# A hybrid decoder block: a third output tile in attention, another order of PSUM banks, two copies' engine, and a Newton step in two operations

## The chip, the cores and the metric
The kernel runs on one core of a Trainium2 chip. The metric is the device time of one execution in microseconds (us). Three executions of the kernel before took 2113.8, 2116.68 and 2114.82 us: a median of 2114.82.

The core's engines run side by side, each through its own list of instructions in order: TensorE (PE, matmuls; its weight loads are shown apart as PEld), VectorE (DVE), ScalarE (ACT), GpSimd (POOL) and SyncE (SP), which here only issues DMAs. ACT and POOL issue DMAs as well.

## The reference
One layer of a decoder block over 2048 positions of width 1024, in float32:

```python
proj = x @ w_in + b_in                      # q, k, v, g_attn, u_lru, g_lru, gate_logits
q, k = rope(q), rope(k)                     # 3 head groups of 8 heads, 64 wide
for g, (window, dilation) in enumerate(((128, 1), (512, 4), (2048, 16))):
    o_g, lse_g = dilated_band_attention(q[:, :, g], k[:, :, g], v[:, :, g], window, dilation)
attn = sum(softmax(lse over g) * o_g) * silu(g_attn)
y_a = attn @ w_attn_proj
u = causal_depthwise_conv(u_lru, conv_w, conv_b)
h = rg_lru(u, ...)                          # block-diagonal gates, a scan over the positions
y_b = (h * silu(g_lru)) @ w_lru_proj
merged = sigmoid(gates[0]) * y_a + sigmoid(gates[1]) * y_b
out = merged @ w_out + b_out
x = layer_norm(alpha * x + out, ln_gain, ln_bias)
```

In each group the positions are regrouped by their residue modulo the dilation, and each block of 128 queries sees its own block of keys and the one before it, cut to a band. For group 2 (dilation 16) there is only one block in each residue, so no block before.

## The kernel before, in words
All five engines' lists are written in program order: the schedule is by hand, and an instruction that waits holds up everything behind it on its engine. Products that need float32 accuracy are done as three matmuls of a high and a low part. `later(n, fn)` puts a step off by `n` rounds; `run(late)` runs what has come due.

**In-projection (to about 1444 us).** Blocks of `x` and of the weights are combined into seven products for eight; one product after the other runs in a ring of `q` tiles (L622) in the first four PSUM banks, those of the pool `ps` that come first; behind them lie the tags `t` and `g`, two banks each. After each product `evacuate` sums it into `y` tiles (DVE, L227), and chains of further steps go on with them: `qk_chain` with the rotation, others with `v`, and `mg_chain` with the merge gates, a `tanh` and a store to `mg_scr`. The SBUF tiles of 2 KB a partition for all of these are 32 slots `s0` to `s31`, taken by `take` and returned by `give`. `take` picks the slot that has been vacant the longest, but for names with `y` in the last step of the plan it goes by the list `LATE` first, each of its slots once; these `y` tiles are the last merge gates', which ACT stores (L386).

**Attention (about 1444 to 1655 us).** The SBUF and the PSUM of the in-projection are released and taken anew by the pools `p_p`, `at_p`, `Y` and `aps`. There are 12 units, one for each head pair `hp` and group, in the order of groups 0, 2, 1; each has four rounds of four query blocks, 48 rounds (`NG`) in all. For round `i`:

- `scores(i)`: matmuls into four `s` tiles, a PSUM bank each (L1005), two at a time. In the first round of a unit it also takes the unit's statistics tile `sta` (three buffers in turn) and its output tile `ot` (8 KB a partition, two buffers in turn).
- `peak`: DVE adds the mask, writes `p` and keeps the row's largest value in `sta` (L1012, eight in a round). `expo`: ACT takes the exponential of `p` and its sum (L1020, eight).
- `turn`: PE transposes `p` into tiles `pt` with the PSUM tag `t`, a bank each (L1030). `bring`: copies of these from PSUM to `ptb` in SBUF, four in a round, by ACT (L1043) or by DVE (L1045). `light` says whether DVE does the one of them that is otherwise ACT's in the second half of the round.
- `values`: matmuls of `ptb` with the values into `o`, of the tag `t` too (L1058).
- `leave`: DVE copies `o` to the unit's `ot` (L1067 in group 0, L1071 in group 2, L1069 in group 1). A round later SP issues the stores: of groups 0 and 1 each quarter of `ot` to `o_scr` (L1073), of group 2 the whole tile once at the end of the unit (L1075); and at the end of each unit the statistics to `st_scr` (L1080, 1082, and for group 1 four at L1085).

The four `s` tiles take four banks and the tag `t` the other four; which of them come first follows from which tag is asked for first. Rounds overlap: the loop's turn `i` holds the scores of round `i`, the second half of the softmax of `i - 1`, `values(i - 2)` and `leave(i - 3)`, in an order that is written out. The loop has three turns without scores at the end (`i` from 48 to 50). Beside it the next units' queries, keys and values are loaded and split in two by POOL (L811), and the last rounds load `h` and the first weights of the next stage.

**Last stages (about 1655 to 2112 us).** The pool `fp` takes PSUM: `y` of four banks for the two projections (`yb`, L1310 to L1312, and `ya`, L1388 to L1390), `ct` of one and `z` of three for the combination of the groups and the out-projection. `out_job` runs 16 times: PE makes `z` from `merged` and `wo` (L1420 to L1422), DVE adds the residual, takes mean and variance; ACT takes a square root, DVE the reciprocal and one Newton step for 1/sqrt(variance + eps) on one column of `mv` (L1451 to L1453), scales and shifts `x` (L1457), and the row is stored. At the end of the last one only DVE, ACT and the stores are left.

Of the kernel before, what the change touches and what calls it, by code (L numbers as in the profile page):

```python
# [8 lines left out]
F32 = mybir.dt.float32  # L9
F32R = mybir.dt.float32r  # L10
AF = mybir.ActivationFunctionType
ALU = mybir.AluOpType
# [3 lines left out]
P = 128  # L16
S = 2048
# [3 lines left out]
CH = 512  # L21
# [10 lines left out]
def hybrid_block_kernel(ctx: ExitStack, tc: tile.TileContext, a: dict, out: bass.AP):  # L32
    nc = tc.nc
    sp, act, dve, pool, pe = nc.sync, nc.scalar, nc.vector, nc.gpsimd, nc.tensor
# [90 lines left out]
    sl_p = stA.enter_context(tc.tile_pool(name="sl_p", bufs=1))  # L125
    ps = stA.enter_context(tc.tile_pool(name="ps", bufs=2, space=PSUM))
    NS, NL = 32, 4
    LATE = [31, 7, 8, 9, 30]
    TRACE = False
    vacant = list(range(NS))  # L130
    home = {}
# [416 lines left out]
    light = [("v", FT_V + 2 * j, FT_V + 2 * j + 1) for j in range(6)]  # L548
# [157 lines left out]
    for s, pl in enumerate(plan):  # L706
        if pl[4] == "ug" and not (pl[0] and pl[1][1][0] - FT_U in put_off):
            at(base[s] + 1, lambda i=pl[1][1][0] - FT_U: fetch_gr(i))
        if pl[0] and pl[4] == "ug":
            i = pl[1][1][0] - FT_U  # L710
# [38 lines left out]
    def bring(t, b, c):  # L749

        at(t - 3, lambda: [keep_raw(b, c, kk) for kk in K4])
        at(t, lambda: [one_block(b, kk) for kk in K4])
# [36 lines left out]
    def unit(u):  # L789

        return (0, 2, 1)[u % 3], u // 3
# [170 lines left out]
    at_p = stB.enter_context(tc.tile_pool(name="at_p", bufs=2, reuse_waits="tile"))  # L962
    Y = stB.enter_context(tc.tile_pool(name="Y", bufs=1, reuse_waits="tile"))
    aps = stB.enter_context(tc.tile_pool(name="aps", bufs=2, space=PSUM, reuse_waits="tile"))
    def prev(g, n):
        if g == 0:
            return n - 1 if n >= 1 else None
        if g == 1:
            return n - 4 if n >= 4 else None
        return None  # L970
# [3 lines left out]
    sta, ot = {}, {}  # L974
# [6 lines left out]
    def scores(i):  # L981
        u, q = divmod(i, 4)
        g, _ = unit(u)
        A, B = units[u]
        if q == 0:
            sta[u] = p_p.tile([P, 16, 4], F32, tag="sta", name=f"sta{u}", bufs=3)
            ot[u] = at_p.tile([P, S], F32, tag="ot", name=f"ot{u}")
        for w in range(2):
            s = st["s", i, w] = [aps.tile([P, 2, 256], F32, tag="s", name=f"s{i}{w}{h}", bufs=4) for h in range(2)]
            for j in range(2):  # L990
                n = 4 * q + 2 * w + j
                lo = first(i, 2 * w + j)
                for x, y in ((0, 0), (1, 0), (0, 1)):
                    for h, hs in enumerate(HALF):
                        K = B[hs, y]
                        if g == 2:
                            k = K.rearrange("p (c r j) -> p r c j", c=4, r=16)[:, n]
                        elif lo:
                            k = K[:, n * P:(n + 1) * P]
                        elif g == 0:  # L1000
                            k = K[:, (n - 1) * P:(n + 1) * P]
                        else:
                            c, r = divmod(n, 4)
                            k = K[:, (c - 1) * CH:(c + 1) * CH].rearrange("p (c r j) -> p r c j", c=2, r=4)[:, r]
                        pe.matmul(s[h][:, j, lo:256], A[hs, x, n * P:(n + 1) * P], k, start=(x + y == 0), stop=(y == 1))  # L1005
# [109 lines left out]
    NG = 48  # L1115
# [4 lines left out]
    for i in range(NG + 3):  # L1120
        u = i // 4
        on, turns = i < NG, 0 < i <= NG
        run(late)
        if i in VORD:
            loads += v_parts(*VORD[i])
        if i % 4 == 0 and 1 <= u <= 9:
            loads += unit_parts(u + 2)
        for _ in range(2):
            if loads:
                loads.pop(0)()  # L1130
        copied = 1 < i <= NG + 1
        light = copied and (unit((i - 2) // 4)[0] == 2 or i % 3 == 1)
        if on:
            scores(i)
        if i > 2:
            leave(i - 3)
        if copied:
            bring(i - 2, 1, 1, dve)
            if light:
                bring(i - 2, 1, 0, dve)  # L1140
        if turns:
            expo(i - 1, 2, 1)
        if copied and not light:
            bring(i - 2, 1, 0, act)
        if turns:
            expo(i - 1, 3, 0)
            expo(i - 1, 3, 1)
        if on:
            peak(i, 0, 0)
            expo(i, 0, 0)  # L1150
            for j, h in ((0, 1), (1, 0), (1, 1)):
                peak(i, j, h)
        if turns:
            turn(i - 1, 0)
            bring(i - 1, 0, 0, act)
            bring(i - 1, 0, 1, dve)
        if on:
            for j, h in ((0, 1), (1, 0), (1, 1)):
                expo(i, j, h)
            peak(i, 2, 0)  # L1160
            peak(i, 2, 1)
        if i > 1 and i - 2 < NG:
            values(i - 2)
        if turns:
            turn(i - 1, 1)
        if on:
            peak(i, 3, 0)
            peak(i, 3, 1)
            expo(i, 2, 0)
        if i in (40, 41):  # L1170
            prep_wl(i - 40, 2)
        if 42 <= i < 46:
            load_h(0, 2 * (i - 42), 2)
            load_h(0, 2 * (i - 42) + 1, 2)
        if i in (46, 47):
            prep_wl(i - 44, 2)
        now["n"] += 1
# [7 lines left out]
    Z = ctx.enter_context(tc.tile_pool(name="Z", bufs=1, reuse_waits="tile"))  # L1185
    rc_p = ctx.enter_context(tc.tile_pool(name="rc_p", bufs=4, reuse_waits="tile"))
    fp = ctx.enter_context(tc.tile_pool(name="fp", bufs=2, space=PSUM, reuse_waits="tile"))
    stC = ctx.enter_context(ExitStack())
    cb_p = stC.enter_context(tc.tile_pool(name="cb_p", bufs=3, reuse_waits="tile"))
    wt_p = stC.enter_context(tc.tile_pool(name="wt_p", bufs=1, reuse_waits="tile"))  # L1190
# [218 lines left out]
    def out_job(tt):  # L1409
        rows = slice(tt * P, (tt + 1) * P)  # L1410
        x = XR.pop(tt)
        mh, ml = MS.pop(tt)
        last = tt == 15
        parts = [slice(0, CH), slice(CH, CH + 256), slice(CH + 256, D)] if last else [slice(0, CH), slice(CH, D)]
        zz = [fp.tile([P, CH], F32, tag="z", name=f"z{tt}{n}", bufs=3)[:, 0:hs.stop - hs.start] for n, hs in enumerate(parts)]
        for k0, k1 in ((0, 6), (6, 8)) if tt == 0 else ((0, 8),) if tt % 4 else ((0, 7), (7, 8)):
            for z, hs in zip(zz, parts):
                for k in range(k0, k1):
                    w = WO[k]
                    pe.matmul(z, mh[:, k], w[:, 0, hs], start=(k == 0), stop=False)  # L1420
                    pe.matmul(z, mh[:, k], w[:, 1, hs], start=False, stop=False)  # L1421
                    pe.matmul(z, ml[:, k], w[:, 0, hs], start=False, stop=(k == 7))  # L1422
        if tt + 1 < 16:
            load_xr(tt + 1)
            split_m(tt + 1, slice(0, 8 if (tt + 1) % 4 else 7))
        if tt == 1:
            for fn in at1:
                fn()
        dve.scalar_tensor_tensor(out=x, in0=x, scalar=ALPHA, in1=vec[0], op0=ALU.mult, op1=ALU.add)
        st_ = cst.tile([P, 4, 6], F32, tag="st", name=f"st{tt}", bufs=2)  # L1430
        n = 0
        for z, hs in zip(zz, parts):
            dve.tensor_tensor(out=x[:, hs], in0=x[:, hs], in1=z, op=ALU.add)
            step = 256 if last else CH
            for q in range(hs.start, hs.stop, step):
                dve.bn_stats(out=st_[:, n, :], in_=x[:, q:q + step])
                n += 1
        mv = cst.tile([P, 4], F32, tag="mv", name=f"mv{tt}", bufs=2)
        dve.bn_aggr(out=mv[:, 0:2], in_=st_[:, 0:n])
        act.activation(mv[:, 2:3], mv[:, 1:2], AF.Sqrt, bias=epst)  # L1440
        halves = (slice(0, CH), slice(CH, D))

        def centre(hs):
            dve.scalar_tensor_tensor(out=x[:, hs], in0=x[:, hs], scalar=mv[:, 0:1], in1=vec[1][:, hs],
                                     op0=ALU.subtract, op1=ALU.mult)

        centre(halves[0])
        dve.reciprocal(out=mv[:, 2:3], in_=mv[:, 2:3])

        dve.tensor_scalar(out=mv[:, 1:2], in0=mv[:, 1:2], scalar1=EPS, scalar2=-0.5, op0=ALU.add, op1=ALU.mult)  # L1450
        dve.tensor_tensor(out=mv[:, 3:4], in0=mv[:, 2:3], in1=mv[:, 2:3], op=ALU.mult)  # L1451
        dve.tensor_scalar(out=mv[:, 3:4], in0=mv[:, 3:4], scalar1=mv[:, 1:2], scalar2=1.5, op0=ALU.mult, op1=ALU.add)
        dve.tensor_tensor(out=mv[:, 2:3], in0=mv[:, 2:3], in1=mv[:, 3:4], op=ALU.mult)  # L1453
        for hs, eng in zip(halves, (sp, act) if last else (act, act)):
            if hs.start:
                centre(hs)
            dve.scalar_tensor_tensor(out=x[:, hs], in0=x[:, hs], scalar=mv[:, 2:3], in1=vec[2][:, hs],  # L1457
                                     op0=ALU.mult, op1=ALU.add)
            eng.dma_start(out[rows, hs], x[:, hs])
# [96 lines left out]
```

## Time and profile before
| | |
|---|---|
| median of the three executions | 2114.82 us (2113.8 to 2116.68) |
| the profiled execution | 2113.77 us |
| its span in the trace | 2112.0 us |
| granted TensorE clock, mean | 0.997 |
| busy PE | 2088.6 us (99%) |
| busy DVE | 1663.8 us (79%) |
| busy ACT | 1120.5 us (53%) |
| busy POOL | 491.9 us (23%) |
| moved by DMA | 524.69 MB, 248 GB/s on average |

The time of an execution is that of the whole program; the span runs from the first to the last record of the trace, and the difference, 1.8 us here, lies around it. An engine's busy time counts the instructions that compute; waiting and issuing are not in it. The table by windows gives for each stretch the same busy times, so that a stage can be read apart from the whole, with the clock that TensorE was granted (1.00 is full speed). A row of an instruction has its start in us from the beginning of the span, its length, its engine and line, what it writes and reads by the program's names, and in brackets how long the engine stood idle just before it and what ended that. "L1071" is line 1071 of the kernel before; in the changed kernel the lines behind the in-projection stand one to three further down.

### The profile page before, as it was taken

The page shows a single profiled execution, that of the slowest core. Times are in us where ns is not written, and L with a number is a line of the kernel's source. Part 1 is how long each engine was busy: PE and PEld are TensorE (multiplying, and loading weights), DVE is VectorE, ACT ScalarE, POOL GpSimd, SP SyncE. Part 2 cuts the span into 40 slices and gives each one's busy share as a digit, 9 for nine tenths or more (in the row PEclk, how much of TensorE's full clock was granted, in tenths as well). Part 3 has the DMA queues.
Part 4 walks back from the last instruction along what each step waited for, and adds up shares of the span by engine and source line. Part 5 has one row for each costly group of instructions (what it writes and reads, how often), then busy time and mean ns, then how long its engine had stood idle before and what let it go on. Part 6 is the DMA issues. An engine that isn't in the chain of part 4 may idle for free.

```text
span 2112.0 us, 35853 instructions
## 1 busy us (share of the span) xinstructions
PE 2088.6 (99%) x12016; PEld 1729.0 (82%) x12016; DVE 1663.8 (79%) x3193; ACT 1120.5 (53%) x2348; POOL 491.9 (23%) x465
## 2 busy tenths in 40 slices
PE   8999999999999999999999999999999999999998
PEld 7888888888888888887888888888989888888887
DVE  8987888888888867787787887877989645576667
ACT  6356456457356565656567666667999411221100
POOL 1111111111111002231232232222536444331120
PEclk9999999999999999999999999999999999999999
DMA  8987997997997976677788788879998788864432
GB/s 271 268 273 223 276 284 209 284 289 234 273 291 237 329 221 200 213 238 212 249 252 274 255 251 269 257 223 382 296 303 263 238 283 274 302 245 155 161 110 70
DMA packets 345832, 524.69 MB, mean 248 GB/s; under 512 B 124208, under 2 KB 153904, under 8 KB 341808
## 3 DMA queue, kind: packets, MB, share of 16 engines
q1 hardware_dynamic: 325760, 489.54, 71.5%
q0 software_dynamic: 12256, 19.42, 5.5%
q10 hardware_dynamic: 7632, 13.44, 1.7%
q8 instruction: 96, 1.57, 0.3%
q14 instruction: 88, 0.72, 0.1%
HBM read 317.14 MB, written 190.45 MB: 240 GB/s over the span
## 4 chain that ended last, share of the span: by engine, by line
PE 91%; ACT 6%; DVE 2%; DMA 1%; issue 0%; SPq 0%
PE q L622 66%; ACT p L1020 5%; PE yb L1310 3%; PE yb L1311 3%; PE z L1420 3%; PE z L1421 3%; PE z L1422 3%; PE yb L1312 3%; PE ya L1388 1%; PE ya L1389 1%; PE ya L1390 1%; PE g L492 1%; PE vtp L358 1%; ACT ptb L1043 1%; PE o L1058 1%; DVE p L1012 1%
## 5 line engine op out<-in xcount | busy, mean ns | idle before, releaser
L622 PE MATMUL q<-xT,hS 128*128 128x512 f32 x1680 | 521.1, 391 | 0.0
L622 PE MATMUL q<-xT,l 128*128 128x512 f32 x1120 | 436.0, 389 | 0.0
L622 PE MATMUL q<-xB,hA 128*128 128x512 f32 x1248 | 389.1, 393 | 5.6 <-ACT xB L215 5.6
L622 PEld LDWEIGHTS q<-xT,hS 128*128 128x128 f32 x1680 | 312.8, 188 | 69.0 <-issue 5.5
L622 PE MATMUL q<-xB,l 128*128 128x512 f32 x904 | 353.0, 390 | 0.0
L622 PEld LDWEIGHTS q<-xB,hA 128*128 128x128 f32 x1248 | 233.7, 189 | 57.0 <-ACT xB L215 5.6
L622 PEld LDWEIGHTS q<-xT,l 128*128 128x128 f32 x1120 | 210.3, 188 | 44.1
L622 PEld LDWEIGHTS q<-xB,l 128*128 128x128 f32 x904 | 170.2, 188 | 36.3 <-DVE l L227 0.5
L1020 ACT ACTIVATE p<-p,sta 128x256 f32<-128x256 f32 (+1 forms) x384 | 175.7, 511 | 5.0 <-DVE sta L1012 4.8
L245 POOL DMA_DIRECT2D wS<-in_w_in_dram x70 | 62.0, 965 | 492.6 <-DMA wS<-in_w_in_dram 137.5
L622 PE MATMUL q<-xB,hS 128*128 128x512 f32 x560 | 174.0, 392 | 0.0
L622 PE MATMUL q<-xT,hA 128*128 128x512 f32 x560 | 173.0, 390 | 0.0
L269 ACT ACTIVATE hA<-wA 128x512 fp32r<-128x512 f32 x218 | 134.9, 623 | 55.4 <-DMA wA<-in_w_in_dram 19.8
L269 ACT ACTIVATE hS<-S 128x512 fp32r<-128x512 f32 x175 | 109.0, 623 | 76.4 <-DVE S L227 48.8
L227 POOL TENSOR_TENSOR S<-S,wA 128x512 f32<-128x512 f32 x35 | 45.6, 1304 | 392.3 <-DVE S L227 218.2
L622 PEld LDWEIGHTS q<-xT,hA 128*128 128x128 f32 x560 | 104.7, 188 | 23.0 <-issue 1.5
L622 PEld LDWEIGHTS q<-xB,hS 128*128 128x128 f32 x560 | 104.0, 188 | 22.4 <-issue 1.5
L1012 DVE CUSTOM_DVE_ANT_0 p<-s,mask 128x256 f32<-128x256 f32 (+1 forms) x384 | 116.7, 363 | 1.3 <-PE s L1005 0.9
L1421 PE MATMUL z<-wo,mh 128*128 128x512 f32 (+1 forms) x264 | 101.0, 383 | 0.0
L1422 PE MATMUL z<-wo,ml 128*128 128x512 f32 (+1 forms) x264 | 101.0, 383 | 0.0
L1420 PE MATMUL z<-wo,mh 128*128 128x512 f32 (+1 forms) x264 | 101.0, 383 | 0.0
L1310 PE MATMUL yb<-h,wl 128*128 128x512 f32 x256 | 100.2, 392 | 0.0
(201 smaller groups left out, 4262.9 us busy)
## 6 DMA issues: line engine op xcount, KB each, us to landing
wA<-in_w_in_dram SPq DMA_DIRECT2D x253, 256.0 KB, 4.8
wl_scr<-l SPq DMA_DIRECT2D x105, 512.0 KB, 5.2
l<-wl_scr SPq DMA_DIRECT2D x105, 512.0 KB, 4.8
sw<-y SPq DMA_DIRECT2D x384, 64.0 KB, 3.3
wS<-in_w_in_dram SPq DMA_DIRECT2D x70, 256.0 KB, 4.8
wS<-in_w_in_dram POOLq DMA_DIRECT2D x70, 256.0 KB, 6.4
qh_scr<-hi SPq DMA_DIRECT2D x48, 256.0 KB, 5.6
v_scr<-vs SPq DMA_DIRECT2D x48, 256.0 KB, 4.8
```

Of the source, the lines that this page charges most:

```text
L227: eng.tensor_tensor(out=out, in0=in0, in1=in1, op=op)
L245: pool.dma_start(t, w_part(s, x), accum_op=ALU.add)
L269: act.activation(h, r, AF.Copy)
L622: pe.matmul(bank, w[:, ks], x[:, kk, xx], start=(first and i == 0), stop=(last and i == 11))
L1012: dve.tensor_tensor_reduce(out=st["p", i, j][:, h, lo:256], in0=st["s", i, j // 2][h][:, j % 2, lo:256], in1=mask[:, lo:256], scale=1.0, s ...
L1020: act.activation(p, p, AF.Exp, scale=-1.0, bias=s[:, h:h + 1], accum_out=s[:, 2 + h:3 + h])
L1310: pe.matmul(yb, WL[f][:, 0, k], xx[:, 0], start=(k == 0), stop=False)
L1311: pe.matmul(yb, WL[f][:, 0, k], xx[:, 1], start=False, stop=False)
L1312: pe.matmul(yb, WL[f][:, 1, k], xx[:, 0], start=False, stop=(k == 7))
L1420: pe.matmul(z, mh[:, k], w[:, 0, hs], start=(k == 0), stop=False)
L1421: pe.matmul(z, mh[:, k], w[:, 1, hs], start=False, stop=False)
L1422: pe.matmul(z, ml[:, k], w[:, 0, hs], start=False, stop=(k == 7))
```

## The change
It has six edits:

- `LATE` has seven slots, 7 to 13, in place of 31, 7, 8, 9 and 30.
- The tag `t` of `aps` is declared ahead of the loop, and so comes first in PSUM: `pt` and `o` get the banks that `q` had, and `s` those behind them.
- `ot` has three buffers in place of two. What follows it in SBUF moves up by 8 KB.
- `light` holds in turn 48 as well, and from turn 47 on the first `bring` of the second part goes to DVE in place of ACT: three copies in all change their engine, one in turn 47 and two in turn 48.
- The tags `ct` and `z` of `fp` are declared ahead of `y`, so that in the last stages `y` gets the banks behind them.
- The Newton step takes two operations of one column where it took three.

```diff
-    LATE = [31, 7, 8, 9, 30]
+    LATE = [7, 8, 9, 10, 11, 12, 13]
...
     aps = stB.enter_context(tc.tile_pool(name="aps", bufs=2, space=PSUM, reuse_waits="tile"))
+    aps.tile([P, 4, P], F32, tag="t", name="t", bufs=4)
...
             sta[u] = p_p.tile([P, 16, 4], F32, tag="sta", name=f"sta{u}", bufs=3)
-            ot[u] = at_p.tile([P, S], F32, tag="ot", name=f"ot{u}")
+            ot[u] = at_p.tile([P, S], F32, tag="ot", name=f"ot{u}", bufs=3)
...
         copied = 1 < i <= NG + 1
-        light = copied and (unit((i - 2) // 4)[0] == 2 or i % 3 == 1)
+        light = copied and (unit((i - 2) // 4)[0] == 2 or i % 3 == 1 or i == NG)
...
             turn(i - 1, 0)
-            bring(i - 1, 0, 0, act)
+            bring(i - 1, 0, 0, act if i < NG - 1 else dve)
             bring(i - 1, 0, 1, dve)
...
     fp = ctx.enter_context(tc.tile_pool(name="fp", bufs=2, space=PSUM, reuse_waits="tile"))
+    fp.tile([P, 4, P], F32, tag="ct", name="ct", bufs=1)
+    fp.tile([P, CH], F32, tag="z", name="z", bufs=3)
...
         dve.tensor_scalar(out=mv[:, 1:2], in0=mv[:, 1:2], scalar1=EPS, scalar2=-0.5, op0=ALU.add, op1=ALU.mult)
-        dve.tensor_tensor(out=mv[:, 3:4], in0=mv[:, 2:3], in1=mv[:, 2:3], op=ALU.mult)
-        dve.tensor_scalar(out=mv[:, 3:4], in0=mv[:, 3:4], scalar1=mv[:, 1:2], scalar2=1.5, op0=ALU.mult, op1=ALU.add)
-        dve.tensor_tensor(out=mv[:, 2:3], in0=mv[:, 2:3], in1=mv[:, 3:4], op=ALU.mult)
+        dve.scalar_tensor_tensor(out=mv[:, 3:4], in0=mv[:, 2:3], scalar=mv[:, 2:3], in1=mv[:, 1:2], op0=ALU.mult, op1=ALU.mult)
+        dve.tensor_scalar(out=mv[:, 2:3], in0=mv[:, 3:4], scalar1=1.5, scalar2=mv[:, 2:3], op0=ALU.add, op1=ALU.mult)
```

## The prediction
> **What bounds the kernel now.** I read the busy shares first, then TensorE's waits, then the same stretches one after another in the table by windows, and last the order of time around the longest wait. The page:
>
> ```profile
> span 2112.0 us, 35853 instructions
> PE 2088.6 (99%) x12016; PEld 1729.0 (82%) x12016; DVE 1663.8 (79%) x3193; ACT 1120.5 (53%) x2348; POOL 491.9 (23%) x465
> ```
>
> TensorE (PE) is busy but for 23 us, so whatever the change can bring lies in those 23 us and in time that PE spends slowed down. The waits of PE over the whole span, the larger ones:
>
> ```profile
> PE q L622 <- ACT xB L215: 5.6, 1, 5.6
> PE pt L1030 <- DVE ot L1071: 3.4, 1, 3.4
> ...
> PE pt L1030 <- DVE ot L1069: 1.1, 1, 1.1
> PE s L1005 <- DVE y L227: 0.5, 1, 0.5
> ```
>
> The 5.6 us are the start of the program, which the change doesn't touch. The other three stand where three of its edits are: 3.4 us behind a copy into an `ot` tile, 1.1 us at the end of attention, 0.5 us at its start. Now the stretches (engine columns are busy time with instruction counts; then the granted clock, the DMA share and GB/s):
>
> ```profile
> 1446.00:1573.00 127.00, 123.76 (x2241) 113.19 (x2239) 123.39 (x597) 127.00 (x535) 56.01 (x61) 1.00 0.94 329
> 1573.00:1577.00 4.00, 0.57 (x11) 0.43 (x9) 0.80 (x2) 1.10 (x6) 0.00 (x0) 1.00 0.60 70
> 1578.00:1584.00 6.00, 6.00 (x64) 5.55 (x62) 5.03 (x33) 5.06 (x25) 1.05 (x2) 0.50 1.04 416
> 1655.00:2104.00 449.00, 448.88 (x2008) 371.99 (x2006) 275.62 (x455) 67.34 (x115) 122.77 (x86) 1.00 0.62 206
> ```
>
> Attention (from about 1445 to 1655) is a different machine from the rest: in its first 127 us ScalarE (ACT) has no idle time at all and VectorE (DVE) and PE are at 97%. Then everything stands for 4 us, and PE afterwards runs at half clock for 6. After 1655 PE has no gap to the last tile, so time saved in attention comes off the end of the span, as long as nothing in the last stages was due by the clock.
>
> **The third `ot` tile.** Units of four rounds take `ot` buffers in turn. Unit 7 (the first with L1071 after the stall) takes with two buffers the one of unit 5, with three that of unit 4. The four copies of unit 3, of unit 4, the last one of unit 6 and the four of unit 7, then the store that unit 5's buffer waited for longest and its landing (each row from an answer of its own: count, shortest/median/longest ns, first and last start; or start and length):
>
> ```profile
> L1067 DVE COPY ot<-o x4: 690/696/700, 1506.3 to 1518.9; 128x512 f32<-128x512 f32 x4
> L1071 DVE COPY ot<-o x4: 687/689/689, 1522.2 to 1533.1; 128x512 f32<-128x512 f32 x4
> 1568.71 0.69 DVE L1067 COPY ot<-o 128x512 f32<-128x512 f32 x1 [0.67 <-PE o L1058]
> L1071 DVE COPY ot<-o x4: 685/688/692, 1576.2 to 1589.0; 128x512 f32<-128x512 f32 x4
> L1073 SPq DMA_DIRECT2D o_scr<-ot x1: 320/320/320, 1564.1 to 1564.1; - x1
> DMA to landing us min/median/max: 12.0/12.0/12.0
> ```
>
> Unit 5's last store was issued at 1564.1 and took 12.0 us to land: 1576.1, and the copy of unit 7 starts at 1576.2. From the last copy of the unit before to the first of this one are 7.5 us, where unit 4 shows 3.3: the wait costs 4.2. The four copies then span 12.8 us, where unit 4 shows 10.9: 1.9 more, in which the half clock falls. Together 6.1. The buffer that unit 7 gets instead was unit 4's, whose one store is issued in the rounds after 1533.1; even with 17 us to land (below) it is free by 1556, long before 1572.0, where the copy would now come. Its row, and below it ACT's waits between 1566 and 1600 (total, times, longest):
>
> ```profile
> L1075 SPq DMA_DIRECT2D o_scr<-ot x1: 320/320/320, 1538.8 to 1538.8; - x1
> DMA to landing us min/median/max: 16.8/16.8/16.8
> ACT p L1020 <- DVE sta L1012: 4.3, 2, 3.7
> ACT ptb L1043 <- PE pt L1030: 0.8, 1, 0.8
> ```
>
> The other bound is ACT, without a gap until then: in 1566 to 1600 it idles 4.3 + 0.8 = 5.1 us, and if ACT alone sets the pace no more than that can come back. I take 5.8, nearer to the measured rounds, because the loss is seen there directly; ends 5.1 and 7.1 (4.1 of waiting and, from the row at clock 0.50, 3.0 if every matmul were on the path).
>
> The rule to weigh here is the Trainium skill's, page "TensorE: Matmul & The Clock Gate", Part 1: after about one idle window of 3.4 us the clock falls to half, and the penalty is the throttled time times one less the clock share. The trace agrees on the cause, a 3.4 us gap and then 0.50, and on no other gap. On the price it doesn't: by the rule the half clock alone cost 3.0 us and the sum below would be -6.7, by the rows it cost 1.9; the rule holds for PE by itself, and here two other engines share the pace.
>
> What is late next: the first peak of unit 8 writes a `sta` tile that unit 5's statistics stores leave free.
>
> ```profile
> L1085 SPq DMA_DIRECT2D st_scr<-sta x4: 525/1208/2882, 1565.4 to 1571.5; - x4
> DMA to landing us min/median/max: 5.4/9.3/10.9
> 1581.06 0.29 DVE L1012 CUSTOM_DVE_ANT_0 p<-s,mask 128x128 f32<-128x128 f32 x1 [0.22 <-ACT p L1020]
> ```
>
> The last is issued at 1571.5 and lands 5.4 later, at 1576.9. That peak came at 1581.06, 0.2 of it idle; 4.2 earlier is 1576.6. I charge 0.2 (ends 0 and 0.9). The buffers move everything behind `ot` in SBUF by 8 KB, which is what the new `LATE` list answers: the tiles that the last `mg_chain` stores read now lie under `ot` buffers 1 and 2, first written tens of us later. Cost nothing; the cover is that distance.
>
> **Banks.** Stage A's `q` ring came first in PSUM, and so did `s`: the wait of 0.5 us for `DVE y` is scores(0) on the bank of the last product. With `t` declared first, `s` lies where `t` and `g` were. PE's 0.5 us go, but ACT has the last gate and its store to issue first:
>
> ```profile
> 1445.36 0.33 ACTq L386 DMA_DIRECT2D mg_scr<-y  x1
> 1445.84 0.40 ACT L1020 ACTIVATE p<-p,sta 128x128 f32<-128x128 f32 x1 [0.52 <-DVE sta L1012]
> ```
>
> ACT is free at 1445.69 and starts at 1445.84, so 0.15 comes through to the engine that sets the pace (ends 0 and 0.5). In stage C declaring `ct` and `z` first keeps `y` on the banks of `s`, free before the last values; without that, `yb` would wait for the last copies (0.7 each). Nothing gained or lost.
>
> **The last rounds' copies.** Three copies leave ACT for DVE: one in round 47, ahead of four peaks, two in round 48. What happens there:
>
> ```profile
> 1645.70 0.69 DVE L1045 COPY ptb<-pt 128x512 f32<-128x512 f32 x1
> 1646.31 0.42 DVE L1012 CUSTOM_DVE_ANT_0 p<-s,mask 128x256 f32<-128x256 f32 x1
> ...
> 1647.68 0.69 DVE L1069 COPY ot<-o 128x512 f32<-128x512 f32 x1
> ...
> 1649.52 1.97 PE L1058 MATMUL o<-ptb,V 128*64 128x128 f32 x32 [0.39 <-ACT ptb L1043]
> ```
>
> A copy takes DVE 0.60 from start to start, and DVE runs without a gap up to here. The one in round 47 moves `leave(45)` from 1647.68 to 1648.28, and with it PE's transposes that wait for its bank (1.1 us now, 1.7 then). In round 48 DVE copies `ot` to 1648.9, ptb to 1649.5, and then the one that ACT had ready for PE's 1649.52, to 1650.1: values(46) starts 0.6 later, and so do the copies and values(47) behind it. So this edit costs 0.6. Ends: a gain of 0.4, all that PE waits there for ACT, and a loss of 1.8, three copies wholly exposed. What ACT is relieved of lies where it isn't last.
>
> **The Newton step.** Three one-column operations become two in 16 tiles. In 15 DVE waits for PE's `z` next, and they cost nothing; only the last tile's are on the path.
>
> ```profile
> 2105.99 0.16 DVE L1451 TENSOR_TENSOR mv<-mv 128x1 f32<-128x1 f32 x1
> 2106.19 0.21 DVE L1452 TENSOR_SCALAR mv<-mv 128x1 f32<-128x1 f32 x1
> 2106.44 0.16 DVE L1453 TENSOR_TENSOR mv<-mv 128x1 f32<-128x1 f32 x1
> 2106.63 0.75 DVE L1457 SCALAR_TENSOR_TENSOR x<-x,mv,vec 128x512 f32<-128x512 f32 x1
> ```
>
> They take 0.64. Both new ones read a scalar from a tile, as L1452 does, which takes 0.25 to the next: 0.50, a gain of 0.14 (ends 0.12 and, at 0.19 like the others, 0.26).
>
> **Sum:** -5.8 + 0.2 - 0.15 + 0.6 - 0.14 = -5.3 us. The profiled execution took 2113.77 (span 2112.0 and 1.8 around it), so 2108.5 for one like it; it is the lowest of the executions shown, 1.05 below their median of 2114.82. Against the median I predict 2109.5.
>
> **Rivals.**
> *It gives more.* If matmuls alone set the pace after the stall, 7.1 come back instead of 5.8, and if ACT is last at the end, its copies' move gains 0.4 instead of costing 0.6: 2.3 more, 2107.2. For it: half clock for 6 us. Against: the measured rounds, and DVE without a gap at the end.
>
> *The next transfer takes the place.* Unit 9's keys are split by POOL until 1590.6, and its scores start at 1597.53, 6 us earlier in the new run:
>
> ```profile
> 1589.34 1.29 POOL L811 TENSOR_TENSOR B<-B 128x512 fp32r<-128x512 f32 x1
> 1597.53 1.69 PE L1005 MATMUL s<-B,A 64*128 64x128 f32 x23
> ```
>
> Margin 0.9 us. With loads that land 3 us later than here (landings of 5 to 17 us stand above) 2 to 2.5 are lost again: 2112. Against: DMA was at 0.60 in the stall, and gets work sooner now.
>
> *The wait stays.* The copy's wait was for something that a third buffer doesn't free: then only the small terms act, 0.6 - 0.3, 2115.1. Against: the landing at 1576.1 and the start at 1576.2.
>
> *Slower.* The seven `LATE` slots are reused while a store of their former tile is still under way, so a last `y` waits for its landing, and the first scores behind it. The last four of these stores took, from issue to landing, up to the third number here:
>
> ```profile
> DMA to landing us min/median/max: 6.7/7.2/8.3
> ```
>
> 8.3 us; that much wait, and the 3.0 of a half clock after it: +11.3 - 5.3 = +6.0, 2120.8. It decides from a wait of 5.3 us on, counting the clock. Against: no VectorE wait for a DMA stands among the waits of this stage, with slots drawn from the same pool.
>
> **How the numbers follow.** A difference of 0.2% (4.2 us) is about what a measurement of this kernel can tell from no change: faster means below 2110.6. Chances: my forecast 0.63, with its own range 2108.2 to 2110.7 from the ends of its terms taken one at a time; more 0.11; next transfer 0.13; wait stays 0.08; slower 0.05. Of the forecast some 0.55 lies below 2110.6, with the 0.11 that is 0.66 faster; slower 0.04, as a short wait there ends within; the same 0.30. The range runs from 2106.6, below the case that gives more, to 2112.6, past the next transfer; the wait that stays and the slower case are left out.
>
> **What would show it.** In the changed profile: no L1071 copy with an idle time of over 1 us and no clock of 0.50 inside attention; the first L1071 of unit 7 3.3 us behind the last L1067; the first peak of unit 8 with 0 to 1 us idle; PE's wait for `DVE y` gone and ACT's first exponential near 1445.7; PE's wait behind L1069 grown from 1.1 to 1.7 and `yb` following some 5 us earlier than now; two rows for three at the end. Wrong I'd be most of all if another landing stops DVE or PE within the same 20 us, or if another gap of over 3 us brings the half clock back.

## The result, and the profile after
The changed kernel took 2110.76 us, median of 14 executions (2108.31 to 2115.74), beside 2115.14 us, median of 14 of the kernel before (2113.8 to 2116.68): a ratio of 0.9978, 95% interval 0.9971 to 0.9985, 4 us faster. Predicted were 2109.5, between 2106.6 and 2112.6, with 0.66 on faster by over 0.2%; it is 0.22%, just past that mark, and the interval reaches down to 0.15%. The profiled execution took 2108.31 (span 2106.5); for one like it the sum had said 2108.5.

The head of the page, and behind it PE's larger waits over the whole span (total, times, longest); lines behind the in-projection now stand one to three further down:

```profile
span 2106.5 us, 35836 instructions
PE 2085.8 (99%) x12016; PEld 1725.9 (82%) x12016; DVE 1665.0 (79%) x3180; ACT 1119.7 (53%) x2345; POOL 492.1 (23%) x465
```

```profile
PE q L622 <- ACT xB L215: 5.6, 1, 5.6
PE pt L1031 <- ACT ptb L1044: 2.0, 5, 0.7
PE o L1059 <- ACT ptb L1044: 1.8, 7, 0.3
PE pt L1031 <- DVE ot L1070: 1.6, 1, 1.6
PE o L1059 <- DVE ptb L1046: 0.4, 1, 0.4
```

The 3.4 us behind an L1071 copy and the 0.5 us for `DVE y` are gone; the wait at the end of attention has grown from 1.1 to 1.6. The same stretches as before (length; busy time of PE, PEld, DVE, ACT, POOL with counts; granted clock, DMA share, GB/s):

```profile
1446.00:1573.00 127.00, 123.49 (x2237) 112.92 (x2239) 123.64 (x594) 127.00 (x535) 55.93 (x61) 1.00 0.94 328
1573.00:1577.00 4.00, 4.00 (x76) 3.64 (x76) 4.00 (x26) 4.00 (x24) 0.00 (x0) 1.00 0.79 107
1578.00:1584.00 6.00, 5.91 (x100) 5.35 (x101) 6.00 (x29) 6.00 (x29) 2.06 (x3) 1.00 1.05 422
1650.00:2098.00 448.00, 448.00 (x2004) 371.39 (x2003) 272.93 (x439) 67.42 (x115) 126.60 (x90) 1.00 0.63 207
```

From 1573 to 1577, where everything stood, all three engines are now busy throughout, and the six microseconds behind it run at full clock. The last copy of unit 6, the first of unit 7, and the first peaks of units 8 and 9, by start and length; then unit 7's four copies together:

```profile
1568.58 0.69 DVE L1068 COPY ot<-o 128x512 f32<-128x512 f32 x1 [0.68 <-PE o L1059]
...
1571.86 0.69 DVE L1072 COPY ot<-o 128x512 f32<-128x512 f32 x1
...
1576.41 0.28 DVE L1013 CUSTOM_DVE_ANT_0 p<-s,mask 128x128 f32<-128x128 f32 x1
...
1593.85 0.29 DVE L1013 CUSTOM_DVE_ANT_0 p<-s,mask 128x128 f32<-128x128 f32 x1 [0.64 <-ACT ptb L1044]
```

```profile
L1072 DVE COPY ot<-o x4: 685/685/685, 1571.9 to 1582.8; 128x512 f32<-128x512 f32 x4
```

Unit 7's first copy comes 3.3 us behind the one before it, and the four span 10.9, both as unit 4 showed before. New is the 0.64 us in front of unit 9's first peak. To see where the time went in every kernel, I cut each trace at the same events: the first exponential (ACT), the first peak of unit 8, of unit 9, the first exponential of unit 11, the first `yb` matmul, the end of the last `z` matmul, the end of the span. Each number is a difference of two times in one trace.

| us | first exp. at | to unit 8 | to 9 | to 11 | to `yb` | to last `z` | to the end |
|---|---|---|---|---|---|---|---|
| before | 1445.84 | 135.22 | 18.36 | 33.54 | 21.64 | 449.28 | 8.11 |
| changed | 1445.59 | 130.82 | 17.44 | 33.55 | 21.81 | 449.28 | 8.04 |
| changed, again | 1446.09 | 131.94 | 17.53 | 33.52 | 21.82 | 449.29 | 8.03 |
| third tile alone | 1446.53 | 130.96 | 17.06 | 33.54 | 21.66 | 449.28 | 8.11 |
| all but the third tile | 1446.99 | 136.58 | 20.13 | 33.56 | 23.42 | 449.29 | 8.03 |
| four `sta` | 1447.22 | 130.68 | 16.72 | 33.63 | 23.65 | 449.38 | 8.02 |
| no last copies | 1446.03 | 130.68 | 17.42 | 33.55 | 21.62 | 449.31 | 8.03 |
| no last copies, again | 1445.58 | 130.68 | 17.90 | 33.55 | 21.62 | 449.26 | 8.03 |
| four `sta`, turn 48 only | 1445.89 | 132.12 | 16.72 | 33.54 | 21.24 | 452.81 | 8.03 |
| the same, again | 1446.48 | 130.69 | 16.72 | 33.71 | 21.35 | 452.16 | 8.03 |
| old `LATE` | 1446.35 | 130.67 | 17.70 | 33.54 | 23.45 | 449.27 | 8.03 |
| `y` first in the last stages | 1446.65 | 131.09 | 17.35 | 33.53 | 21.94 | 449.28 | 8.04 |
| changed, repeated transposes | 1449.47 | 131.28 | 17.68 | 33.55 | 21.81 | 450.16 | 8.02 |
| before, repeated scores | 1446.19 | 135.70 | 19.24 | 33.55 | 21.60 | 451.33 | 8.12 |

From before to changed: -0.25, -4.40, -0.92, +0.01, +0.17, 0, -0.07: together -5.46. Many entries repeat to a few hundredths, so a difference of 0.1 can be read where nothing waits for a DMA. The in-projection itself ends anywhere between 1443.7 and 1447.6 in these traces, in kernels of both kinds; that column says nothing of the change. One execution of the third tile alone took 3585.56 us; it is in no ratio below, and the record gives no reason for it.

### The profile page after: what moved, and what is told of

Read it like the earlier page. It is cut to its first block, busy times and chain, and to the rows that moved or that the text cites. A ratio compares the mean times of both kernels' runs of the same rounds, so it can differ in the third digit from the quotient of the medians.

```text
span 2106.5 us, 35836 instructions
## 1 busy us (share of the span) xinstructions
PE 2085.8 (99%) x12016; PEld 1725.9 (82%) x12016; DVE 1665.0 (79%) x3180; ACT 1119.7 (53%) x2345; POOL 492.1 (23%) x465
## 5 line engine op out<-in xcount | busy, mean ns | idle before, releaser
L1021 ACT ACTIVATE p<-p,sta 128x256 f32<-128x256 f32 (+1 forms) x384 | 180.0, 577 | 0.7 <-DVE sta L1013 0.7
L1021 ACT ACTIVATION_READ_ACCUMULATOR p<-p,sta 128x1 f32 x384 | 119.2, 317 | 0.0
```

The costliest lines, as they stand in the source:

```text
L1021: act.activation(p, p, AF.Exp, scale=-1.0, bias=s[:, h:h + 1], accum_out=s[:, 2 + h:3 + h])
```

## The experiments
**The third tile alone, and all the rest without it.**

```diff
-    LATE = [31, 7, 8, 9, 30]
+    LATE = [7, 8, 9, 10, 11, 12, 13]
-            ot[u] = at_p.tile([P, S], F32, tag="ot", name=f"ot{u}")
+            ot[u] = at_p.tile([P, S], F32, tag="ot", name=f"ot{u}", bufs=3)
```

> The kernel before with the third ot buffer and the new LATE list, nothing else. Theory (the stall was unit 7's copy waiting for unit 5's stores; of 6.0 us that come back, 0.6 are lost again where unit 9's first peak waits for unit 6's statistics store to land): span 5.2 to 5.6 us shorter than before (2106.4 to 2106.8), median near 2110.9, no clock of 0.50 in attention, the start 0.2 later than in the changed kernel. Rival (the gain comes from the banks or the last copies): less than 1 us of it, above 2114.

Median 2110.57 us, ratio 0.9977 (0.9967 to 0.9987): all of the gain, with the `LATE` list, which goes with the tile (below it is undone by itself). Span 2107.1, 0.3 above the range, by its later in-projection (first exponential 0.7 later than before). The other kernel is the changed one with these two lines put back:

> The changed kernel with two ot buffers and the old LATE list. Theory: the 4.1 us of waiting in front of unit 7's first copy and the half clock stand again; -0.2 at the start, +0.16 at the end of attention, -0.1 in the last tile: span 2111.8 to 2112.0, median within 0.5 of before. Rival (the small edits carry a part of the gain): 2 us or more below before.

Median 2117.23, ratio 1.0009 (1.0000 to 1.0018): nothing of the gain is left, and at 2.1 us above the kernel before it misses the 0.5 expected. The profiled execution is a long one, with a span of 2118.0. The waits with two tiles are there, but at other places than in the first trace. DVE's three longest waits from 1500 to 1600, PE's longest stop there, then two stretches at the end of attention:

```profile
DVE ot L1070 <- DMA o_scr<-ot: 2.6, 1, 2.6
DVE ot L1072 <- PE s L1006: 1.9, 1, 1.9
DVE p L1013 <- PE s L1006: 1.5, 1, 1.5
```

```profile
1525.72 1.00 PE L1006 MATMUL s<-B,A 64*128 64x128 f32 x14 [1.69 <-issue]
```

```profile
1650.34:1653.75 3.41, 1.77 (x41) 1.46 (x39) 3.41 (x12) 3.41 (x15) 3.25 (x5) 1.00 0.82 210
1653.76:1657.16 3.40, 3.40 (x37) 3.28 (x35) 1.92 (x4) 0.04 (x1) 3.24 (x5) 0.50 0.27 96
```

Unit 7's copy waits 1.9 us (the trace has no landing of unit 5's last store, and names the scores), and unit 8's 2.6 for unit 6's stores. Which unit waits how long changes from one execution to the next, but in all three traces with two tiles some unit does. Two things here are not the `ot` tile's. PE's scores of round 19 stop for 1.7 us at a place where the trace sees nothing to wait for ("issue"); with the two steps of half clock behind it, from 1527.5 to 1534.3, the way from unit 3's last copy to unit 5's first takes 23.0 us in place of 18.8. That is 4.2 of the 5.8 us by which this trace reaches unit 8 later than the changed kernel's first, so the column "to unit 8" must not be read as the price of two tiles. And in the last row, behind the longer wait at the end of attention, PE runs 3.4 us at half clock; the way to `yb` takes 23.42 us where the changed kernel's first trace has 21.81.

**The statistics tile, and the changed kernel once more.**

```diff
-            sta[u] = p_p.tile([P, 16, 4], F32, tag="sta", name=f"sta{u}", bufs=3)
+            sta[u] = p_p.tile([P, 16, 4], F32, tag="sta", name=f"sta{u}", bufs=4)
```

> The changed kernel with four sta buffers in place of three: unit 9 then takes the statistics tile of unit 5. Theory (unit 9's first peak waits 0.64 us for the landing of unit 6's statistics store): the wait goes, span 0.6 shorter than the changed kernel's 2106.5, and if it is this landing that makes the executions of the changed kernel differ by several us, a median 1 to 2 us lower and a narrower spread. Rival (the 0.64 us belong to ScalarE, which the trace names as the releaser): the same time as the changed kernel.

> The changed kernel once more, for a second trace and for times on the same chip. Median 2110 to 2111.5. Theory (its executions differ by the landing of the statistics store): a slower profiled execution shows a longer wait in front of unit 9's first peak, and nothing else. Rival (they differ by the in-projection or by the half clock elsewhere): the wait is the same, and the difference stands at another place.

Medians 2110.85 (0.9978, 0.9968 to 0.9988) and 2110.2 (0.9977, 0.9968 to 0.9986). The wait is the landing's. In the changed kernel's first trace, unit 6's statistics store:

```profile
L1081 SPq DMA_DIRECT2D st_scr<-sta x1: 371/371/371, 1580.6 to 1580.6; - x1
DMA to landing us min/median/max: 13.1/13.1/13.1
```

Issued at 1580.56, landed at 1593.69, and the peak starts at 1593.85, 0.16 behind it. In six more traces with three buffers that show this landing (the changed kernel again, the third tile alone, both without the last copies, the one with `y` first, and the one with repeated transposes) the distance is 0.16 or 0.17. With four buffers the same peak, at the same place, waits for nothing, and the stretch from unit 8 to unit 9 takes 16.72 in all three traces, against 17.06 to 17.90 with three; the 0.64 us were not ScalarE's, which the row names. The changed kernel's second trace has 0.71 in front of unit 9's peak and shows the same at unit 8, as a wait for unit 5's statistics:

```profile
1578.03 0.29 DVE L1013 CUSTOM_DVE_ANT_0 p<-s,mask 128x128 f32<-128x128 f32 x1 [1.15 <-DMA st_scr<-sta]
```

Four buffers thus remove what was 0.7 us of waiting in the first trace and 1.9 in the second. Yet the median is no lower and the spread no narrower (2107.78 to 2115.64): what makes the executions differ is not this landing alone. In its profiled execution the half clock came at the end of attention.

**The half clock at the end of attention.** PE's busy time (the number behind the length) in the stretch of 3.41 us in which the wait behind the `ot` copy lies, and in the next; four tables, of the kernel with four `sta` tiles, of the changed kernel's first and its second trace, and of the one without the three copies.

```profile
1642.03:1645.44 3.41, 1.77 (x40) 1.51 (x38) 3.41 (x12) 2.96 (x13) 3.25 (x5) 1.00 1.05 413
1645.45:1648.85 3.40, 3.40 (x37) 3.07 (x34) 1.59 (x4) 0.00 (x0) 3.24 (x4) 0.50 0.56 74
```

```profile
1641.71:1645.12 3.41, 1.77 (x36) 1.60 (x35) 3.41 (x13) 2.22 (x10) 3.33 (x4) 1.00 0.66 130
1645.13:1648.53 3.40, 2.96 (x56) 2.48 (x54) 2.65 (x5) 0.00 (x0) 3.24 (x4) 1.00 0.69 147
```

```profile
1641.29:1644.70 3.41, 2.23 (x45) 1.92 (x41) 3.41 (x15) 3.41 (x15) 3.25 (x5) 1.00 1.06 371
1644.71:1648.11 3.40, 2.94 (x59) 2.71 (x61) 3.08 (x6) 0.92 (x4) 3.24 (x5) 1.00 0.51 54
```

```profile
1640.62:1644.03 3.41, 2.13 (x46) 1.69 (x42) 3.15 (x12) 3.41 (x14) 3.25 (x4) 1.00 1.04 325
1644.04:1647.44 3.40, 3.22 (x60) 2.98 (x62) 1.78 (x3) 1.59 (x6) 3.24 (x5) 1.00 0.40 45
```

In each trace the clock's changes lie on a grid of 3.413 us, at a phase of its own, and the half clock lasts one or two steps. Where the wait of 1.64 us falls into one step, PE is busy for 1.77 of 3.41, and in three of four such traces the next step is at half clock (four `sta`, all but the third tile, old `LATE`; the changed kernel's first trace is the fourth). Where a border cuts the wait (two traces) it is not. Where it is 1.1 us long, as without the copies, it is not either, in any of seven traces. Two experiments change the wait. First the copies undone:

```diff
-        light = copied and (unit((i - 2) // 4)[0] == 2 or i % 3 == 1 or i == NG)
+        light = copied and (unit((i - 2) // 4)[0] == 2 or i % 3 == 1)
-            bring(i - 1, 0, 0, act if i < NG - 1 else dve)
+            bring(i - 1, 0, 0, act)
```

> The changed kernel without its three copies on VectorE at the end of attention. Theory (the copies lengthen PE's wait behind the last but two ot copy from 1.1 to 1.64 us, which costs 0.16 us by itself, and in two of the four traces with them a stretch of 3.41 us at half clock follows, which costs 1.85 more): PE's wait is 1.1 again, from the first exponential of unit 11 to yb 21.65 us, no clock of 0.50 there in any profile, and a median 0.5 to 1 us below the changed kernel's. Rival (half clock there has another cause, or the copies pay): the half clock appears all the same, or the median is the changed kernel's or higher.

> The changed kernel without its three copies on VectorE once more, beside the next one on the same chip. If the copies of the changed kernel cost it some 1 us in the middle of its executions: median 2109 to 2110 again, 21.6 us from the first exponential of unit 11 to yb, no half clock there. If the first sample was chance: about 2110.7, as the changed kernel.

Medians 2109.43 (0.9974, 0.9963 to 0.9984) and 2110.16 (0.9981, 0.9972 to 0.9989): the stretch to `yb` is 21.62 twice and the clock stays, as expected, but the median that was to be 0.5 to 1 us lower is not: by their ratios the times do not tell the two kernels apart. Second, the wait filled with work:

```diff
-        for j in js:
+        for j in js * (3 if (i, w) == (46, 1) else 1):
             for x in range(first(i, j) // P, 2):
```

> The changed kernel with the 16 transposes of the second half of round 46 run three times into the same tile: 1.4 us of PE work more, which lies in PE's wait of 1.64 us. Theory (the half clock comes from that idle time): the wait is 0.2 to 0.3, yb starts as before, 21.8 us behind the first exponential of unit 11, and no half clock follows in any profile; median 0.5 to 1 us below the changed kernel's in spite of the added work. Rival (a clock that drops by chance): half clock there in about half of the profiles, the same median or a higher one.

The wait was 0.7 us long (not 0.2: the repeated transposes took less than I had added up), the clock stayed, `yb` came at 21.81. The median of 2111.15 (0.9982, 0.9973 to 0.9991) is not the lower one I expected; its profiled execution ended the in-projection at 1447.6, 2 us or more behind the others, with a step of half clock in it, and lost 0.9 in the last stages. One trace agrees with the theory; it is not a proof.

**The copy of turn 47 apart from those of turn 48**, with four `sta` tiles:

```diff
-            bring(i - 1, 0, 0, act if i < NG - 1 else dve)
+            bring(i - 1, 0, 0, act if i < NG else dve)
```

> The changed kernel with four sta buffers, and of the three copies only those two of turn 48 on VectorE; turn 47's stays on ScalarE. Theory (the copy of turn 47 makes the wait longer, the two of turn 48 take away values(46)'s wait for ScalarE): PE's wait behind the ot copy 1.1, no wait of values(46) for ScalarE, 21.2 to 21.4 us from the first exponential of unit 11 to yb; no wait for st_scr; attention 202.2 to 202.6 us from the first exponential to yb against 203.6 to 204.8 in the changed kernel; median about 2108.5 to 2109.5. Rival (waits of other transfers take the place, or ScalarE hides it): attention no shorter than 203.6.

> Four sta buffers and only turn 48's copies on VectorE, once more. In its own stretches it is the shortest of all, 1.4 us under the changed kernel's trace; if the late loads of unit 5's keys and of the last stages are chance, its median comes out at 2108.5 to 2109.5, below no_tail's; if four sta buffers bring such late loads with them, its trace has a wait of the scores at unit 5 again and the median stays near 2110.5.

To `yb` 21.24 and 21.35: shorter than before (21.64) and than changed (21.81), so turn 48's copies gain 0.3 to 0.4 and turn 47's loses 0.5. It has the lowest execution of all, 2106.79 us, but the medians are 2110.47 (0.9979, 0.9970 to 0.9987) and 2109.9 (0.9979, 0.9970 to 0.9988): no gain on the changed kernel that these runs can show. The first trace stops PE's scores for 1.2 us, the second does not. I had called that late keys of unit 5; the traces say otherwise. It is in round 19, unit 4's last, the matmul waits for no semaphore, and it is the same matmul that stops for 1.7 us in the trace of all but the third tile and for 1.0 in that with the repeated transposes. Both have three `sta` tiles, so the fourth does not bring it. In these three traces the packets of the DMA queue that the profile calls "instruction" (q8) end 1.2 to 1.4 us before this matmul starts, in the eleven others at least 1.6 before: a late load of instructions fits, but no run tests it.

Both traces lose about 3 us in the last stages, 452.81 and 452.16 against 449.28. PE's waits there in the second one, 1.6 us of its 2.9:

```profile
PE z L1425 <- DVE ml L1410: 0.8, 1, 0.8
PE ya L1391 <- DVE gA L1396: 0.6, 1, 0.6
PE z L1423 <- ACT mh L1409: 0.2, 1, 0.2
```

The merge gates `gA` come by DMA. This edit is not needed for that lateness: the changed kernel's two traces do not have it, but the one with repeated transposes waits 0.6 us for `ml`, and the next experiment, a form of the kernel before, 0.8. Whether the edit makes it more frequent stays open.

**The stall's half clock by itself**, in the kernel before: PE repeats matmuls while it would wait.

```diff
-            for j in range(2):
+            for j in (0, 1) * (3 if (i, w) == (31, 1) else 1):
                 n = 4 * q + 2 * w + j
```

> The kernel before with the scores of the second half of round 31 run three times into the same tiles: 2.8 us of PE work more, in front of the transposes that wait for unit 7's first copy. The copy's wait for unit 5's stores stays. Theory (the half clock behind the stall costs 1.9 of the 6.0 us): no clock of 0.50 there, and from unit 7's first ot copy to the first peak of unit 9 21.3 us in place of 23.2; the span 1.9 shorter than before where the wait is 4.1 long. By the rule of throttled time the price would be 3.0: 20.2 us. Rival (the two other engines set the pace and the clock costs nothing): 23.2 us as before.

Median 2116.66, ratio 1.0007 (0.9997 to 1.0016). The profile is inconclusive. The copy waited 4.1 us as before, but PE still idled 2.1 of them and one step of half clock followed instead of two; then unit 8's copy waited as well:

```profile
DVE ot L1071 <- DMA o_scr<-ot: 4.1, 1, 4.1
DVE ot L1069 <- DMA o_scr<-ot: 2.4, 1, 2.4
```

```profile
1577.70:1581.08 3.38, 3.31 (x35) 2.86 (x35) 3.37 (x22) 2.46 (x12) 0.00 (x0) 0.50 0.81 286
```

From unit 7's first copy (1577.02) to unit 9's first peak (1601.13) are 24.1 us, or 21.7 if the new wait counts in full; before it was 23.2. By that, half of the half clock gone gave back 1.5. The first row also names what the profile of before had left as "issue": the copy's wait was for `o_scr<-ot`, the stores.

**The two lists that should cost nothing.** The changed kernel with the old `LATE`, and without the lines that declare `ct` and `z` first:

> The changed kernel with the old LATE list. Theory (the cover is the distance of tens of us between the last gate's stores and the first writes of ot and of what lies above it): the same stretches, the first exponential 1.89 us behind the last product. Rival (with the buffers moved up by 8 KB, an early tile of attention lies on a slot whose store is still under way): a wait for mg_scr of up to several us in the first 20 us of attention.

> The changed kernel without the tags ct and z declared first in the last stages' pool: y takes the banks that the tag t has in attention. Theory: the first yb waits for the last copies out of these banks, the ot copy that starts 0.1 us after the present yb start: yb 0.5 to 0.8 later, 22.3 to 22.6 us behind the first exponential of unit 11 in place of 21.8. Rival (y's four tiles are asked for slowly enough): 21.8.

Each ran once, in 2110.8 and 2109.59 us. With the old `LATE` nothing waits in the first stretch (130.67), so these seven slots bring no time; whether they matter in other executions, one trace can't say. With `y` on the banks of `t` the first `yb` comes at 21.94, 0.13 later, not 0.5 to 0.8.

## Why the prediction was right, and where not
- **The third tile** carried it, as said. The wait and the half clock: -5.8 predicted; to unit 8's first peak -4.40, from there to unit 9's -0.92 with the new 0.72 in it: -6.0, inside 5.1 to 7.1. The second trace gives the same: -4.1, with 1.9 of new waits in it. From unit 7's first copy to unit 9's first peak it is 23.22 us before and 21.99 after; less the 0.72 the difference is 1.95, and 1.9 was the price set on the half clock.
- **What is late next** was the right kind and the wrong place. I charged 0.2 for unit 8's peak behind unit 5's statistics; there nothing was lost in the first trace and 1.15 in the second, beyond the end of 0.9. Unit 9 behind unit 6's statistics I did not look at. In the kernel before that store landed, by these two views, 5.3 us ahead of the peak:

```profile
L1080 SPq DMA_DIRECT2D st_scr<-sta x1: 371/371/371, 1580.9 to 1580.9; - x1
DMA to landing us min/median/max: 13.2/13.2/13.2
```

```profile
1599.42 0.28 DVE L1012 CUSTOM_DVE_ANT_0 p<-s,mask 128x128 f32<-128x128 f32 x1
```

  The peak moved up by 5.6 and would have by 6.2, the issue by 0.4 (1580.95 to 1580.56): SP waits there for the landing of an earlier `o_scr<-ot` store, 1580.88 before and 1580.50 after, and not for the engines that stood still. The margin could be read from rows of before; checking one unit further would have shown it. The rival of the next transfer had the mechanism too, with 2 to 2.5 lost, but named unit 9's keys, which were in time.
- **Banks:** -0.15 predicted. From the last product to the first exponential 2.00 us in the three traces with the old order, 1.89 in eleven with the new: -0.11. That `yb` would otherwise wait 0.7 was too much: 0.13.
- **The last copies** (three, not the two of the title): +0.6 predicted, +0.17 measured in the undisturbed trace. PE's wait behind `ot` grew to 1.64, by the 0.6 I had worked out. The step that failed is the next one, that values(46) starts 0.6 later as well: it started 0.64 us behind the end of that wait where it had taken 1.10, without the 0.39 for ScalarE. I had let it wait for the copy that DVE makes in ScalarE's place, the second of the four in the row below, 0.6 us each; it began while that one ran. Why it had waited for ScalarE's copy before and does not wait for this one, the traces don't say.

```profile
1643.32 2.47 DVE L1046 COPY ptb<-pt 128x512 f32<-128x512 f32 x4
1643.46 0.71 PE L1031 MATMUL pt<-ident,p 64*128 64x64 f32 x15 [1.64 <-DVE ot L1070]
1644.10 1.97 PE L1059 MATMUL o<-ptb,V 128*64 128x128 f32 x32
```

  And the edit has a second price that I had not foreseen: in three of six traces the half clock behind the longer wait, 1.6 to 1.8 us.
- **Newton:** -0.14 predicted, -0.07 to -0.09 by the last column, below the end of 0.12. The two take 0.50 as said, but the first now reads what the operation ahead of it writes, and starts 0.17 behind that one's start, where L1451, which didn't, stood 0.11 behind.

```profile
2100.48 0.13 DVE L1453 TENSOR_SCALAR mv<-mv 128x1 f32<-128x1 f32 x1
2100.65 0.22 DVE L1454 SCALAR_TENSOR_TENSOR mv<-mv 128x1 f32<-128x1 f32 x1
2100.91 0.21 DVE L1455 TENSOR_SCALAR mv<-mv 128x1 f32<-128x1 f32 x1
2101.15 0.75 DVE L1459 SCALAR_TENSOR_TENSOR x<-x,mv,vec 128x512 f32<-128x512 f32 x1
```

- **The whole:** profile against profile -5.46, predicted -5.3; medians -4.4. Both profiled executions were low ones for their kernel, the changed kernel's the lowest of 14. That the profiles come so near is in part luck: 0.5 us more than charged went to statistics, 0.4 less than charged to the last copies, and 0.14 of the gain is the in-projection's earlier end. Why the medians gained 1 us less stays open. Losses of that size are on record: the statistics waits (0.7 and 1.9 in the changed kernel's two traces), the half clock at the end (1.6 to 1.8 in three of six traces with the three copies, though in neither of these two), and the stop in round 19 (three of fourteen traces). But the kernel with four `sta` tiles and turn 48's copies alone has neither of the first two, and its medians are no lower (though both its traces lose 3 us in the last stages); and the median of the kernel before itself moved from 2115.1 to 2113.74 us between two series on one chip. The rivals: the wait did not stay, nothing waited for a `LATE` slot. The change that gives more did not come either: it had the copies gain 0.4, and they cost 0.17.

## What to carry to other kernels
When a stall goes, everything behind it moves up, but what is issued by a queue that did not stand still does not: take each landing behind the stall, for several units and not only the next, and subtract the time won from its margin. Judge a small change by stretches between events that repeat to hundredths, and look at more than one trace before a price is called fixed: the same wait of 1.64 us cost 0.2 us in three traces and 1.6 to 1.8 more in three. An idle stretch of the matmul engine should be kept well below the length that costs clock (1.58 us and more in one step here), also where another engine's work is balanced by it.

## What the runs showed of the hardware that I had not expected
A PE wait of 1.64 us is enough for half clock. By the steps of the 3.413 us grid in all fourteen traces, the program's two ends left out: with 1.58 us or more idle in one step, the next was at half clock in eight of nine cases (1.58, 1.64 three times, 1.67, 2.02, 2.29 and 2.68; the exception is 1.64 in the changed kernel's first trace); with 1.47 or less, never. How long it lasts they do not settle: two steps behind 2.68 and 1.67, one behind the other six. The Trainium skill, page "TensorE: Matmul & The Clock Gate", Part 1, has a free-running window of 3413 ns, and the grid agrees; that it takes a window idle throughout, a gap of about 3.4 us, these traces contradict. Its price, the throttled time times a half, is 1.7 us for one step; at the end of attention, where PE is busy throughout that step and ACT and DVE are not, 1.6, 1.6 and 1.8 were measured, which agrees, while in the stall two steps (6.83 us, where the prediction had counted 6) cost 1.95 and not 3.4.
